# Summing a residual gate in 16 double pieces, and moving the last stages' tiles by 64 bytes

## The chip, the cores and the metric

The kernel runs on one core of one Trainium2 chip. The metric is the device time of one execution in microseconds; the smaller, the better. Engines are named as in the profile: PE (TensorE, with PEld for its weight loads), DVE (VectorE), ACT (ScalarE), POOL (GpSimd) and SP (SyncE, which issues all the DMAs of this kernel).

## What is computed

One layer of a diffusion backbone on 256 latent and 256 context tokens, 2048 channels wide, in f32:

```
sh_x, sc_x, g_x = split(silu(c) @ w_mod + b_mod, 3)        # the residual gate is g_x, 2048 numbers
hm   = rmsnorm(h) * (1 + scale) + shift                    # latents and context
u    = hm @ w_in    # r, k, v, z, decay, a | q, kv, k_rope, z | merge gates
y    = rwkv7_scan(...) over context then latents, both directions, 16 heads
o_rw = groupnorm(y) + bonus, gated by silu(z)
o_ml = attention of latents over latents + context, gated by silu(z)
m    = sigmoid(mg_r) * (o_rw @ w_br_r) + sigmoid(mg_m) * (o_ml @ w_br_m)
out  = x + g_x * (m @ w_out)
```

## The kernel before

Every big product is made of three matmuls in the float32r type, high part times high part, high times low and low times high (`mm3`, L222). Weights come in 512 KB tiles `w` of a pool with three buffers (`NW`). The generator `weights` (L211) loads one and splits it in two halves, `wh` on ACT and `wl` on DVE. A projection tile (`proj_g`, L359) takes two such loads and makes 48 matmuls of 256 columns for the latents alone, or of 512 for latents and context.

The first stage (to about 137 us) makes the modulation and the normed input `hmh`, `hml`. Then comes the recurrence: 16 halves (8 head pairs, context then latents), each with a `front` that prepares it, a `diagonal` that inverts 16x16 blocks by way of small DRAM tiles (`dl`, `ln`, `dw`, `WT`), and a `back` that carries the state. A planner (`drive`, with a modelled clock) weaves these chains with a background of projection tiles while the program is written; the framework then orders each engine's queue by its own estimate of readiness. Attention follows, then the branch stage (`chp`, 768 matmuls of 256 columns, from 1168 us) and the output stage (`ch`, `lv`, 384 of 512 columns).

The residual gate needs `silu(c) @ w_mod_g`. It is cut in 8 column blocks `b` by 4 row groups `r`. Each piece is one load of 512 KB and four matmuls that lie side by side in TensorE, into the unused half of a projection tile's `acc` bank. `gate_add` sums the pieces of a block in `gacc` on DVE; `gate_sum` (two small matmuls and an addition) makes two columns of `gT`. When all 8 blocks are there, `gd<-gT` stores `gT` transposed to DRAM (2048 runs of four bytes), from where the output stage reads it back as `gx`. The store is written behind the attention in the program; the framework puts it where it becomes ready.

In the program as built, the tiles `hmh` and `hml` begin 64 bytes past a multiple of 128 in each partition, `w`, `wh` and `wl` on a multiple of 128, and so do `ob0h` to `ob1l` (the branches' inputs), `mh` and `mlo` (the merged tile, high and low part).

Of the kernel before, what the change touches and what calls it, by code (L numbers as in the profile page):

```python
# [9 lines left out]
F32 = mybir.dt.float32  # L10
# [6 lines left out]
P = 128  # L17
D = 2048
KT = D // P
T = 256  # L20
# [32 lines left out]
NW, NSP, UN, NWM = 3, 3, 2, 11  # L53
# [74 lines left out]
def hybrid_block(  # L128
# [20 lines left out]
    nc = tc.nc  # L149
    clock = Clock()  # L150
    V, S = Elementwise(nc.vector, clock, 960, 0.066), Elementwise(nc.scalar, clock, 1200, 0.08)
    E = Tensor(nc.tensor, clock)
# [3 lines left out]
    wp = ctx.enter_context(tc.tile_pool(name="wp", bufs=2))  # L156
# [28 lines left out]
    ssil = cst.tile([P, KT, 32], F32, name="ssil")  # L185
# [17 lines left out]
    def halfs(pool, shape, name, bufs=2):  # L203
        return [pool.tile(shape, F32R, name=name + c, tag=name + c, bufs=bufs) for c in "hl"]
# [39 lines left out]
    with tc.tile_pool(name="p1", bufs=2) as p1:  # L244
# [43 lines left out]
        for k in range(KT):  # L288
# [3 lines left out]
            else:  # L292
                V.tensor_tensor(sq, xT[:, k], xT[:, k], ALU.mult)
            g = k % 4
            E.matmul(pst[32 * g:32 * g + 32], lhsT=con("ones")[:, 0:32], rhs=sq, start=k < 4, stop=k >= KT - 4,
                     tile_position=(0, 32 * g))
# [62 lines left out]
    def proj_g(tile_i, n):  # L359

        ps = pp.tile([P, 512], F32, name="acc", tag="acc", bufs=2)
        gate = None
        for q in range(2):
            if not q and n == T and gate_left:
                gate = gate_mm(ps[:, T:TT])
                yield
            for i, (wh, wl) in enumerate(weights(w_proj[tile_i, q], 1024)):
                for k in range(4):
                    cs = slice(128 * k, 128 * k + 128)
                    kk = 8 * q + 4 * i + k  # L370
                    mm3(ps[:, 0:n], wh[:, cs], wl[:, cs], hmh[:, kk, 0:n], hml[:, kk, 0:n], kk == 0, kk == KT - 1)
                    if n > T or k % 2:
                        yield
            if gsum:
                gate_sum()
        if gate:
            gate_add(ps[:, T:TT], *gate)
        return ps[:, 0:n]
# [1 line left out]
    gT = cst.tile([P, KT], F32, name="gT")  # L380


    gate_left = [(b, r) for b in range(8) for r in range(4)]
    gacc = wp.tile([P, T], F32, name="gacc", bufs=1)
    gsum = []

    def gate_mm(ps):

        b, r = gate_left.pop(0)
        wg = wp.tile([P, 4, T], F32, name="w", tag="w", bufs=NW)  # L390
        nc.sync.dma_start(wg, w_mod_g[b, r])
        for g in range(4):
            E.matmul(ps[32 * g:32 * g + 32], lhsT=ssil[:, 4 * r + g], rhs=wg[:, g], start=True, stop=True,
                     tile_position=(0, 32 * g))
        return b, r

    def gate_add(ps, b, r):
        if r:
            V.tensor_tensor(gacc, gacc, ps, ALU.add)
        else:  # L400
            V.tensor_copy(gacc, ps)
        if r == 3:
            gsum.append(b)

    def gate_sum():
# [898 lines left out]


    mg = ctx.enter_context(tc.tile_pool(name="mg", bufs=2))
    ob = [halfs(mg, [P, 8, T], f"ob{b}", 1) for b in range(2)]
    orw = mg.tile([P, 8, T], F32, name="orw", bufs=1)
    for b in range(2):
# [7 lines left out]
    while gate_left:  # L1317
        ps = pp.tile([P, 512], F32, name="acc", tag="acc", bufs=2)
        gate_add(ps[:, 0:T], *gate_mm(ps[:, 0:T]))
# [6 lines left out]
    for j in range(KT):  # L1326
        tm = []
        for b in range(2):
            th = mg.tile([P, T], F32, name=f"gth{b}")
            nc.sync.dma_start(th, thd[16 * b + j])  # L1330
            ps = pp.tile([P, 512], F32, name="chp", tag="ch", bufs=2)
# [150 lines left out]
```

## Time and profile before

| what | value |
|---|---|
| time, median of 3 runs | 1366.77 us (1360.61 to 1370.45) |
| the profiled execution's own time | 1353.92 us |
| its span, first to last instruction | 1351.9 us |
| mean granted TensorE clock | 0.997 |
| PE / PEld / DVE / ACT busy | 1312.3 / 1076.7 / 945.6 / 622.1 us |
| gate pieces | 32 loads, 32 sums on DVE |

PE busy is the union of its matmuls' spans; gaps are what is left. "idle before" and the bracket at a row's end tell how long the engine had stood before it and which instruction let it go. PEclk is the clock that was granted, 1.00 being full. In the timeline a plain f32 matmul of the program shows as two records, so four gate matmuls are `x8`.

### The profile page before, as it was taken

To read this page: it belongs to the slowest core of one execution; us is meant where nothing else is said; L and a number is where in the kernel's file an instruction comes from. 1 tells how busy PE (TensorE), PEld (TensorE's weight loads), DVE (VectorE), ACT (ScalarE), POOL (GpSimd) and SP (SyncE) were. 2 spreads that over 40 slices of the span, in tenths; PEclk is the share of its full clock that TensorE was granted. 3 is DMA by queue.
4 is the path that set the end of the run, shared out by engine and by line. 5 is a ranking of instruction groups with operands and counts; after the bars stand their busy time and mean duration, and the time that the engine had idled before them with its cause. 6 is when DMAs were issued, how large, how long until landed. Compare 5 with 4: busy or idle time off the path is not lost. (4 is left out here: it accounts for less than half of the span.)

```text
span 1351.9 us, 29680 instructions
## 1 busy us (share of the span) xinstructions
PE 1312.3 (97%) x11522; PEld 1076.7 (80%) x11522; DVE 945.6 (70%) x2675; ACT 622.1 (46%) x1370; POOL 3.3 (0%) x9
## 2 busy tenths in 40 slices
PE   5999999999999999999999998999999999999998
PEld 1767877787777877877877887876998888999887
DVE  3444988777877877787687685663488777677655
ACT  2444554444434544444435343433465565444443
POOL 0000000000000000000000000000000000000000
PEclk9999999999999999999999998999999999999999
DMA  9995564244322433433433453321743334877585
GB/s 369 417 388 199 187 175 108 69 143 131 90 77 77 122 96 94 125 91 103 125 83 103 122 138 91 103 83 56 226 149 125 101 95 139 267 227 224 197 270 174
DMA packets 127741, 208.13 MB, mean 154 GB/s; under 512 B 63600, under 2 KB 80752, under 8 KB 127088
## 3 DMA queue, kind: packets, MB, share of 16 engines
q1 hardware_dynamic: 127600, 206.23, 48.7%
q8 instruction: 91, 1.49, 0.5%
q14 instruction: 50, 0.41, 0.1%
HBM read 193.33 MB, written 12.85 MB: 153 GB/s over the span
## 5 line engine op out<-in xcount | busy, mean ns | idle before, releaser
L123 ACT CAST wh<-w 128x512 fp32r<-128x512 f32 (+2 forms) x484 | 291.4, 607 | 327.2 <-PE acc L104 143.8
L123 DVE TENSOR_TENSOR wl<-w,wh 128x512 fp32r<-128x512 f32 (+1 forms) x480 | 322.0, 676 | 168.7 <-ACT wh L123 140.8
L104 PE MATMUL acc<-hmh,wh 128*128 128x256 f32 (+1 forms) x1200 | 385.7, 322 | 0.2 <-ACT wh L123 0.2
L104 PE MATMUL acc<-hml,wh 128*128 128x256 f32 (+2 forms) x1200 | 369.4, 308 | 0.0
L104 PE MATMUL acc<-hmh,wl 128*128 128x256 f32 (+1 forms) x1184 | 364.4, 308 | 1.3 <-DVE wl L123 1.2
L104 PEld LDWEIGHTS acc<-hmh,wh 128*128 128x128 f32 x1200 | 225.8, 188 | 29.4 <-issue 9.1
L104 PEld LDWEIGHTS acc<-hmh,wl 128*128 128x128 f32 x1184 | 222.9, 188 | 15.2 <-DVE wl L123 2.3
L104 PEld LDWEIGHTS acc<-hml,wh 128*128 128x128 f32 (+1 forms) x1200 | 225.3, 188 | 11.1 <-issue 0.2
L123 ACT COPY UV<-Mn 64x128 f32<-64x128 f32 x112 | 33.1, 295 | 33.8 <-DVE Mn L123 32.5
L123 ACT COPY UV<-chp 64x128 f32<-64x128 f32 x64 | 16.5, 258 | 61.9 <-PE chp L104 61.6
L123 DVE TENSOR_TENSOR pr<-wt 64x14 f32<-64x14 f32 (+6 forms) x224 | 42.4, 189 | 2.6
L123 DVE TENSOR_TENSOR wt<-wt,pr 64x14 f32<-64x14 f32 (+6 forms) x224 | 42.2, 188 | 2.5
L123 DVE COPY xs<-chp 128x128 f32<-128x128 f32 x64 | 18.5, 288 | 35.3 <-PE chp L104 33.4
L104 PE MATMUL pm<-wm,ssil 128*32 128x256 f32 x512 | 34.9, 398 | 8.2 <-DMA wm<-in_w_mod_ss 8.1
L104 PEld LDWEIGHTS chp<-UV,AQ 128*64 128x64 f32 (+1 forms) x512 | 24.9, 135 | 19.7 <-issue 6.4
L104 PE MATMUL a<-hmh,wh 128*128 128x512 f32 x96 | 40.6, 423 | 0.0
L104 PEld LDWEIGHTS chp<-UV,BKT 128*64 128x64 f32 x448 | 24.4, 136 | 20.1 <-issue 8.8
L123 DVE SCALAR_TENSOR_TENSOR Mn<-chp,rho,Mr 128x64 f32<-128x64 f32 x96 | 23.5, 279 | 23.9 <-PE chp L104 23.7
L104 PE MATMUL wk<-QR,BK 64*128 64x128 f32 x256 | 37.2, 286 | 2.8 <-DVE QR L123 2.8
L104 PE MATMUL a<-hmh,wl 128*128 128x512 f32 x96 | 38.0, 396 | 0.0
L104 PE MATMUL a<-hml,wh 128*128 128x512 f32 x96 | 37.8, 394 | 0.0
L104 PE MATMUL chp<-UV,BKT 128*64 128x64 f32 x448 | 37.2, 238 | 0.6 <-ACT UV L123 0.4
(324 smaller groups left out, 2484.9 us busy)
## 6 DMA issues: line engine op xcount, KB each, us to landing
w<-in_w_proj SPq DMA_DIRECT2D x148, 512.0 KB, 3.7
wm<-in_w_mod_ss SPq DMA_DIRECT2D x64, 512.0 KB, 9.2
w<-in_w_mod_g SPq DMA_DIRECT2D x32, 512.0 KB, 3.7
w<-in_w_br SPq DMA_DIRECT2D x32, 512.0 KB, 4.3
w<-in_w_out SPq DMA_DIRECT2D x32, 512.0 KB, 3.9
w<-in_w_first SPq DMA_DIRECT2D x16, 384.0 KB, 7.4
xT<-in_xcT SPq DMA_DIRECT2D x4, 1024.0 KB, 12.5
thd<-th SPq DMA_DIRECT2D x32, 128.0 KB, 2.3
```

The lines of the kernel that those rows point to most:

```text
L104: return self.engine.matmul(out, lhsT=lhsT, rhs=rhs, **kw)
L123: return fn(out, *a, **kw)
```

## The change

Each gate piece now takes two loads and eight matmuls: the two groups of four add up in the accumulator, so there are 16 pieces, 16 sums on DVE, and half as many projection tiles carry one. And a tile of 16 floats per partition, `shift`, which nothing uses, is allocated ahead of `ob`, so the tiles of the branch and output stages (`ob`, `orw`, `mh`, `mlo`, `gx` and the small ones) begin 64 bytes further on, 64 past a multiple of 128. `w`, `wh` and `wl` stay.

```diff
-    gate_left = [(b, r) for b in range(8) for r in range(4)]
+    gate_left = [(b, r) for b in range(8) for r in range(2)]
...
         b, r = gate_left.pop(0)
-        wg = wp.tile([P, 4, T], F32, name="w", tag="w", bufs=NW)
-        nc.sync.dma_start(wg, w_mod_g[b, r])
-        for g in range(4):
-            E.matmul(ps[32 * g:32 * g + 32], lhsT=ssil[:, 4 * r + g], rhs=wg[:, g], start=True, stop=True,
-                     tile_position=(0, 32 * g))
+        wgs = []
+        for i in range(2):
+            wgs.append(wp.tile([P, 4, T], F32, name="w", tag="w", bufs=NW))
+            nc.sync.dma_start(wgs[i], w_mod_g[b, 2 * r + i])
+        for i in range(2):
+            for g in range(4):
+                E.matmul(ps[32 * g:32 * g + 32], lhsT=ssil[:, 4 * (2 * r + i) + g], rhs=wgs[i][:, g], start=i == 0, stop=i == 1,
+                         tile_position=(0, 32 * g))
...
-        if r == 3:
+        if r == 1:
             gsum.append(b)
...
     mg = ctx.enter_context(tc.tile_pool(name="mg", bufs=2))
+
+    mg.tile([P, 16], F32, name="shift", bufs=1)
     ob = [halfs(mg, [P, 8, T], f"ob{b}", 1) for b in range(2)]
```

The planner sees other matmuls, so the whole order of the recurrence shifts. Three places matter below. The first is SP's queue where the projections begin; `w<-in_w_mod_g` is a gate load, `w<-in_w_proj` a weight load, and the number behind a name is that of the buffer's use. Before:

```order
L391 DMA w_1478<-in_w_mod_g 128x1024
L214 DMA w_1484<-in_w_proj 128x1024
L214 DMA w_1518<-in_w_proj 128x1024
L391 DMA w_1558<-in_w_mod_g 128x1024
L214 DMA w_1564<-in_w_proj 128x1024
```

Now:

```order
L393 DMA w_1484<-in_w_mod_g 128x1024
L393 DMA w_1486<-in_w_mod_g 128x1024
L214 DMA w_1496<-in_w_proj 128x1024
L214 DMA w_1530<-in_w_proj 128x1024
L393 DMA w_1577<-in_w_mod_g 128x1024
L393 DMA w_1579<-in_w_mod_g 128x1024
```

Four loads per tile now share the three buffers, where it was three; each load takes the buffer of the third load ahead of it, so `w_1530`, a tile's second weight load, takes that of `w_1484`, its first gate load.

The second place is the store of the gate on SP. Before, it stood in the fifteenth half's part, ahead of that half's `dl` and `ln`:

```order
L978 DMA orwd_1298<-y_9684 128x256
L1323 DMA gd_14602<-gT_1289 128x16x1
L214 DMA w_10420<-in_w_proj 128x1024
L795 DMA dl_10178<-AQ_10040 16x8x16 x8
L421 DMA thd_1293<-th_10256 128x256
L214 DMA w_10570<-in_w_proj 128x1024
L798 DMA ln_10248<-dl_10178 64x256
```

Now it stands behind the eighth half's `ln` and ahead of `th<-in_wup`, the small weights of the next pair's decay and gate projections:

```order
L801 DMA ln_5699<-dl_5643 64x256
L214 DMA w_6121<-in_w_proj 128x1024
L214 DMA w_6170<-in_w_proj 128x1024
L1328 DMA gd_14587<-gT_1289 128x16x1
L214 DMA w_6234<-in_w_proj 128x1024
L636 DMA th_6018<-in_wup 128x256
L424 DMA thd_1293<-th_5920 128x256
L819 DMA dw_5785<-wt_5751 64x2x256
```

The store has moved forward by some 180 SP instructions and has other neighbours.

The third place is DVE where that load is used: `wal<-th,wah` is the low part of `th`; `W` (in the code `W2`) and `xs` belong to the `back` chain. Before, in a pair's row:

```order
L123 COPY xs<-chp 128x128
L123 TENSOR_TENSOR wt<-wt,pr 64x8x7
L123 SCALAR_TENSOR_TENSOR rs_z<-rs_y 128x8
L123 TENSOR_TENSOR wal<-th,wah 128x256
L123 TENSOR_TENSOR pr<-wt 64x7x8
L123 TENSOR_TENSOR rs_z<-rs_z,nrm 128x8
```

Now, for the load behind the store:

```order
L123 SCALAR_TENSOR_TENSOR rs_z<-rs_y 128x8
L123 TENSOR_TENSOR wal<-th,wah 128x256
L123 TENSOR_TENSOR wt<-wt,pr 64x3x12
L123 TENSOR_TENSOR W_5850<-WT_1302,lv 128x512
L123 TENSOR_TENSOR pr<-wt 64x2x13
L123 TENSOR_TENSOR rs_z<-rs_z,nrm 128x8
L123 COPY xs<-chp 128x128
```

`W` and `xs`, which the `back` chain's next matmuls need, have come to stand behind `wal`.

## The prediction

> **What bounds the kernel.** I read the page first: its span, the busy times and the chain that ended last.
>
> ```profile
> span 1351.9 us, 29680 instructions
> PE 1312.3 (97%) x11522; PEld 1076.7 (80%) x11522; DVE 945.6 (70%) x2675; ACT 622.1 (46%) x1370; POOL 3.3 (0%) x9
> PE 34%; DMA 3%; DVE 3%; ACT 1%; issue 1%; DVEq 0%; ACTq 0%; SPq 0%
> ```
>
> TensorE is occupied for 97% of the span and leads the chain (which can't be followed past the branch stage's dense part, so its shares do not add up to 100%). So only three things can move the time: TensorE's own work, its 1351.9 - 1312.3 = 39.6 us of gaps, and its clock. Next I read the stretches that the change touches.
>
> ```profile
> core 0: us, PE busy (x) PEld busy (x) DVE busy (x) ACT busy (x) POOL busy (x), PEclk, DMA share, GB/s
> 137.00:200.00 63.00, 59.98 (x506) 52.45 (x502) 55.42 (x151) 30.63 (x62) 1.44 (x4) 1.00 0.59 186
> 200.00:440.00 240.00, 237.43 (x2336) 184.77 (x2337) 183.65 (x578) 104.59 (x253) 0.00 (x0) 1.00 0.36 101
> 800.00:850.00 50.00, 43.30 (x455) 38.34 (x453) 34.85 (x101) 21.38 (x51) 0.00 (x0) 0.93 0.41 111
> ```
>
> From 137 to 440 us, where the gate's loads will now be crowded, TensorE idles for 3.0 and 2.6 us. The largest hole is at 800 to 850: 6.7 us idle, and the only stretch here whose clock falls below 1.00. The SP queue's rows in order of time show who made it.
>
> ```profile
> 808.27 0.92 SPq L1323 DMA_DIRECT2D gd<-gT  x1
> 810.61 0.34 SPq L214 DMA_DIRECT2D w<-in_w_proj  x1
> 811.21 12.31 SPq L795 DMA_DIRECT2D dl<-AQ  x8
> ...
> 825.40 0.46 SPq L798 DMA_DIRECT2D ln<-dl  x1
> ```
> ```profile
> gd<-gT SPq DMA_DIRECT2D x1, 8.0 KB, 13.0
> ```
> ```profile
> 829.36 0.67 DVE L123 COPY wt<-ln 32x256 f32<-32x256 f32 x2 [3.61 <-DMA ln<-dl]
> ...
> 831.86 0.69 DVE L123 TENSOR_TENSOR Z<-lv,cc 128x512 f32<-128x512 f32 x1
> ...
> 832.60 1.65 PE L104 MATMUL lv<-WT,Z 64*64 64x64 f32 x26 [5.85 <-DVE Z L123]
> ```
>
> The gate's transposed store, only 8 KB, takes 13.0 us to land, and the eight `dl` stores behind it take 12.31 us to issue. `ln` comes late, VectorE stands in `wt<-ln` and cannot reach `Z`, and TensorE waits 5.85 us. It then runs slow:
>
> ```profile
> 835.27 0.56 PE L104 MATMUL acc<-hmh,wh 128*128 128x256 f32 x1
> ...
> 836.48 0.41 PE L104 MATMUL acc<-hmh,wl 128*128 128x256 f32 x1
> ```
>
> Five spacings in 1.21 us are 0.24 us each, about twice the pace of other stretches. Of the clock, 0.07 x 50 = 3.5 us is lost; about 1 us of that falls into the wait itself, so the loss is 2.5 us and the hole costs 8.3 us in all.
>
> **Term 1, half as many gate sums.** A gate's four matmuls cost TensorE their own time and two changes of stream.
>
> ```profile
> 159.34 0.28 PE L104 MATMUL acc<-hmh,wl 128*128 128x256 f32 x1
> 159.54 0.64 PE L104 MATMUL acc<-w,ssil 128*32 128x256 f32 x8
> 160.11 0.39 PE L104 MATMUL acc<-hmh,wh 128*128 128x256 f32 x1
> ```
> ```profile
> 61.25 1.93 PE L104 MATMUL pm<-wm,ssil 128*32 128x256 f32 x32
> ```
>
> From the projection matmul ahead of the gate to the one behind it pass 0.77 us, against 0.113 without a gate: 0.66 us for one set. Four sets in a row (the `pm` row: same shapes) take 1.93 us against 0.64 for one, so each added set costs 0.43. Joining two saves 0.66 - 0.43 = 0.23 us, and sixteen joins save **3.6 us**. Bounds: nothing, if the second load is not there in time (term 4), and 5.3 us (16 x 0.33) if the exit shrinks too.
>
> On VectorE sixteen additions go.
>
> ```profile
> L123 DVE TENSOR_TENSOR gacc<-gacc,acc x24: 406/421/422, 151.9 to 788.2; 128x256 f32<-128x256 f32 x24
> ACT th L123 <- DVE gacc L123: 15.1, 13, 2.2
> ```
>
> That is 16 x 0.42 = 6.7 us and about half of ScalarE's 15.1 us of waiting. Both engines have slack beside TensorE, so I count nothing; if TensorE weren't the cover, at most 6.7 us would come back.
>
> **Term 2, the store `gd` moves.** The sums are now complete near the eighth half of the recurrence, not the fourteenth. The store leaves the place above, which frees 8.3 us, and lands two rows ahead of the load `th<-in_wup`. What waits there is seen one pair later in the trace of before:
>
> ```profile
> 583.75 0.43 SPq L633 DMA_DIRECT2D th<-in_wup  x1
> 587.40 0.40 ACT L123 CAST wah<-th 128x256 fp32r<-128x256 f32 x1 [1.79 <-DMA th<-in_wup]
> 589.56 0.41 DVE L123 TENSOR_TENSOR wal<-th,wah 128x256 fp32r<-128x256 f32 x1
> ```
>
> ScalarE already waits for this load, which takes 3.6 us; VectorE needs it 5.8 us after its issue. Behind the store it lands like the `w` of 810.61, 12.6 us after issue, some 9 us late. After 2.2 us of slack VectorE stands 7 us at `wal`, with `W2` and `xs` behind it in the order, for which TensorE waits; TensorE has about 1.5 us queued ahead. So 5.5 us idle and again 2.3 us of clock: 7.8 us. Net **-0.5 us**. Bounds: -8.3, if the order of before and after leaves enough work ahead, and +4, if VectorE's backlog counts too. I take the middle, since the nearest row, the hole of before, has the same make. SP itself stands at the store until the last `gT` is written, and behind it also wait the spill `thd` and the store `dw`; I count nothing for `dw`, because the inversion that feeds it is held at `wal` as well.
>
> **Term 3, the 64 bytes.** Two rows of one unbroken stream in the timeline, with the number of matmuls between them, give the pace of a matmul; the rows with x768 and x96 are the chain's.
>
> ```profile
> 975.83 0.28 PE L104 MATMUL acc<-hml,wh 128*128 128x256 f32 x1
> ...
> 979.00 0.28 PE L104 MATMUL acc<-hmh,wl 128*128 128x256 f32 x1
> ```
> ```profile
> 799.06 0.28 PE L104 MATMUL acc<-hmh,wh 128*128 128x256 f32 x1
> ...
> 802.94 0.28 PE L104 MATMUL acc<-hmh,wh 128*128 128x256 f32 x1
> ```
> ```profile
> 1168.21 92.15 PE chp L104 x768
> ...
> 1282.24 21.76 PE lv L104 x96
> ```
> ```profile
> 600.53 0.39 PE L104 MATMUL acc<-hmh,wh 128*128 128x512 f32 x1
> ...
> 607.53 0.39 PE L104 MATMUL acc<-hmh,wh 128*128 128x512 f32 x1
> ```
>
> With moving tiles at 64 past a multiple of 128 (`hmh`, `hml`) and weights on a multiple, 256 columns take 3.17 / 28 = 0.113 us in most streams and 3.88 / 33 = 0.118 in some. In the branch stage both lie on a multiple, and the pace is 92.15 / 768 = 0.120. With 512 columns it is the reverse: 7.00 / 30 = 0.233 in the first relation, 21.76 / 96 = 0.227 in the output stage, where both lie on a multiple. The change gives both stages the first relation. The branch stage then gains 768 x 0.0067 = **5.1 us** (1.8 at the pace 0.118), the output stage pays 384 x 0.0066 = **2.5 us** (nothing, if only the moving tile counts, since there it is the stationary one that shifts). Nothing covers either: TensorE has no gaps there.
>
> [...]
>
> **Term 4, three buffers for four loads.** Before, the one gate tile's buffer is free a whole tile ahead. Now the tile's second weight load takes the buffer of its own gate load, so it is issued only when that gate has run.
>
> ```profile
> w<-in_w_mod_g SPq DMA_DIRECT2D x32, 512.0 KB, 3.7
> ```
> ```profile
> L123 ACT CAST wh<-w 128x512 fp32r<-128x512 f32 (+2 forms) x484 | 291.4, 607 | 327.2 <-PE acc L104 143.8
> L123 DVE TENSOR_TENSOR wl<-w,wh 128x512 fp32r<-128x512 f32 (+1 forms) x480 | 322.0, 676 | 168.7 <-ACT wh L123 140.8
> ```
> ```profile
> 136.65 0.64 PE L104 MATMUL acc<-w,ssil 128*32 128x256 f32 x8
> ...
> 190.15 0.64 PE L104 MATMUL acc<-w,ssil 128*32 128x256 f32 x8 [0.23 <-ACT th L123]
> ```
>
> Gate 0.7, landing 3.7, issue 0.3, the two halves of a split 0.6 + 0.7: ready 6.0 us after the tile's start. A tile takes (190.15 - 136.65) / 6 = 8.9 us here, of which 48 x 0.113 = 5.4 are its own matmuls, 0.7 its gate and 2.8 other work. TensorE wants the second load after 1.1 + 2.7 + 1.4 = 5.2 us: 0.8 us short. Queued behind it on SP stand the next gate's loads and the next first load, which is ready some 1 us late too; the two overlap in part. Seven tiles at about 1 us, less the 3.0 us of gaps that fall together with it, cost **4 us**. Bounds 0 and 12. After 200 us a tile has about as much other work as its own, so the remaining nine are covered; without that cover each costs 1 to 2.6 us.
>
> **Sum.** -3.6 - 0.5 - 5.1 + 2.5 + 4 = -2.7 us: the profiled execution would go from 1353.92 to 1351.2. The median shown, 1366.77, lies 0.95% above that execution; I take the same difference off it: **1364 us**.
>
> **Rivals.**
> - The store's new place is covered: work queued on TensorE hides the late load, and VectorE's stand costs nothing there. For it: the rest of the recurrence loses only 1 us in 100. Against: ScalarE already waits for this load. Term 2 becomes -8.3: 1356 us.
> - The shift does nothing (the pace follows from how a stream is entered, as the 0.113 and 0.118 of equal tiles hint). [...] Terms 1, 2 and 4 remain: 1366.6 us.
> - On the other side: the loads starve all sixteen double tiles. If other work between gate and second load stays under 1.4 us, each tile pays 1.0 us for its second load and 1.6 us for the next first one: 16 x 2.6 = 42 us in place of 4, and the time is 1402 us. For it: three buffers, four loads a tile. Against: DMA is busy to 0.36 only, and chains fill half of TensorE after 200 us.
>
> **Chances.** Forecast 0.56, covered store 0.18, idle shift 0.15, starved tiles 0.09, none of these 0.02. The range, with the ends of terms 2 to 4 and half a per cent for the runs, is 1350 to 1380. A measurement of this kernel tells about 1% from no change: below 1353 lie a quarter of the covered store and a fifth of the forecast's spread, 0.17; above 1380 the starved tiles and a few slow ends, 0.12; between, 0.71.
>
> **What would show it.** Gate rows `acc<-w,ssil x16` of about 1.05 us (term 1). `gd<-gT` near the middle of the span, `wah` and `wal` late by 7 us behind it, one halved clock there and none near 830 (term 2). `chp` of x768 in 87 us and the four output blocks at 22.4 us each (term 3). More PE idle between 137 and 200, released by `wh` or `wl` (term 4). I'm wrong if a new long wait stands elsewhere in the reshuffled order, or if the branch stage keeps its 92 us.

## The result, and the profile after

| what | before | after |
|---|---|---|
| median of 20 runs each | 1358.78 us (1353.45 to 1370.45) | 1367.59 us (1362.45 to 1378.30) |
| ratio to before, 95% interval | | 1.0056 [1.0031, 1.0080] |
| profiled execution, its span | 1353.92, 1351.9 us | 1367.96, 1365.8 us |
| mean granted clock in that execution | 0.997 | 0.984 |

By the ratio, the change makes the kernel 0.56% slower, about 7.6 us; the two medians lie 8.8 us apart. The forecast was 2.7 us less. The median lies inside the range that was given, but the sign is wrong. The first lines of the page after:

```profile
span 1365.8 us, 29667 instructions
...
PE 1316.4 (96%) x11522; PEld 1083.3 (79%) x11522; DVE 942.8 (69%) x2659; ACT 620.2 (45%) x1370; POOL 3.3 (0%) x9
```

Of the 13.9 us between the two spans 9.8 are gaps of TensorE (49.4 us against 39.6) and 4.1 are longer busy time, though there is less to do. The table of stretches says where; its columns are as in the prediction. First three stretches of before, then the kernel after:

```profile
200.00:240.00 40.00, 39.95 (x419) 31.42 (x420) 32.42 (x98) 17.80 (x41) 0.00 (x0) 1.00 0.39 105
...
440.00:600.00 160.00, 159.19 (x1655) 127.14 (x1652) 122.81 (x410) 72.00 (x174) 0.00 (x0) 1.00 0.37 107
...
960.00:1020.00 60.00, 59.51 (x446) 55.41 (x447) 43.56 (x125) 34.61 (x70) 0.00 (x0) 1.00 0.59 182
```
```profile
137.00:200.00 63.00, 56.28 (x443) 47.91 (x442) 50.65 (x134) 28.17 (x58) 3.09 (x5) 0.92 0.55 181
200.00:240.00 40.00, 37.26 (x355) 30.43 (x354) 25.49 (x88) 13.69 (x30) 0.00 (x0) 0.91 0.48 141
...
440.00:600.00 160.00, 154.58 (x1631) 125.70 (x1631) 117.57 (x361) 71.58 (x173) 0.00 (x0) 0.99 0.39 104
...
800.00:850.00 50.00, 48.28 (x459) 42.66 (x459) 38.94 (x127) 25.98 (x62) 0.00 (x0) 1.00 0.48 140
...
960.00:1020.00 60.00, 57.34 (x417) 54.82 (x416) 37.38 (x103) 30.83 (x62) 0.00 (x0) 0.91 0.61 184
```

From 137 to 240 us TensorE now idles 6.7 + 2.7 us; before it was 3.0 and 0.05. The clock, 1.00 in both stretches before, is 0.92 and 0.91. The hole at 800 to 850 is gone (1.7 us idle in place of 6.7), and one has come between 440 and 600 (5.4 us in place of 0.8). A last one, at 974, has half clock behind it. In all, the clock stood at one half for 30.7 us between 137 us and the output stage's end, before for 6.8. Three places in the timeline, the first at the second tile that carries a joined piece:

```profile
140.13 0.33 SPq L214 DMA_DIRECT2D w<-in_w_proj  x1
140.57 0.85 SPq L393 DMA_DIRECT2D w<-in_w_mod_g  x2
145.67 3.24 SPq L214 DMA_DIRECT2D w<-in_w_proj  x2
```
```profile
144.35 1.30 DVE L123 TENSOR_TENSOR wl<-w,wh 128x512 fp32r<-128x512 f32 x2 [0.59 <-ACT wh L123]
...
150.44 1.14 ACT L123 CAST wh<-w 128x512 fp32r<-128x512 f32 x2 [1.51 <-DMA w<-in_w_proj]
```
```profile
147.88 1.07 PE L104 MATMUL acc<-w,ssil 128*32 128x256 f32 x16
151.10 0.39 PE L104 MATMUL acc<-hmh,wh 128*128 128x256 f32 x1 [2.15 <-ACT wh L123]
```

The gate's two loads hold two of the three buffers. So the tile's first weight load goes out only at 145.67, when `wl` of the tile before is done (144.35 + 1.30) and the third comes free. It lands just ahead of `wh` at 150.44; TensorE runs the 16 gate records, then stands for 2.15 us. That is the shortage of buffers that term 4 spoke of, but on the tile's first load, for which it had counted some 1 us. Not every early gap is of this kind:

```profile
218.77 0.41 PE L108 MATMUL wk<-cc,rnb 128*128 128x128 f32 x2 [1.95 <-DVE rnb L123]
```

Of the 9.5 us idle from 137 to 240 us, the waits over 0.4 us for `wh` and `wl` make 4.8; this one and another behind it, for VectorE's `W`, make 2.7, and no load ends either. The second place is the store:

```profile
498.27 0.38 SPq L1328 DMA_DIRECT2D gd<-gT  x1
499.65 1.25 SPq L214 DMA_DIRECT2D w<-in_w_proj  x1
500.94 0.43 SPq L636 DMA_DIRECT2D th<-in_wup  x1
```
```profile
508.75 0.67 PE L104 MATMUL chp<-UV,AQ 64*64 64x64 f32 x4 [1.93 <-issue]
...
513.00 0.40 ACT L123 CAST wah<-th 128x256 fp32r<-128x256 f32 x1 [6.48 <-DMA th<-in_wup]
513.44 0.42 DVE L123 TENSOR_TENSOR wal<-th,wah 128x256 fp32r<-128x256 f32 x1 [6.50 <-ACT wah L123]
...
514.99 0.45 PE L104 MATMUL chp<-xs,W 64*64 64x64 f32 x8 [1.80 <-DVE xs L123]
```

The load `th<-in_wup` lands 12.1 us after its issue, ScalarE stands 6.48 us, VectorE 6.50 us at `wal`, and `xs` is late for TensorE: the prediction's chain, link by link. The third place had not been foreseen:

```profile
974.92 0.68 DVE L123 TENSOR_TENSOR krw<-krw 64x512 f32<-64x512 f32 x1 [4.18 <-DMA krw<-krd]
975.53 0.67 DVE L123 TENSOR_TENSOR wl<-w,wh 128x512 fp32r<-128x512 f32 x1
976.25 0.38 PE L104 MATMUL acc<-hmh,wl 128*128 128x256 f32 x1 [2.48 <-DVE wl L123]
```

A small load of the attention's keys is late, VectorE stands at it with a `wl` behind it. With joined pieces and no 64 bytes the same gap was 0.90 us in one profiled execution and 2.04 in another (the two kernels `pair_only` and `pair_cheap` below), so its size changes between executions. Last, the chain:

```profile
1181.25 90.46 PE chp L104 x768
...
1294.18 22.40 PE lv L104 x96
```

The branch stage takes 1.7 us less than before (92.15), the output blocks 0.64 us more each (21.76).

### The profile page after: what moved, and what is told of

It reads as the page before. It is cut to its first block, busy times and chain, and to the rows that moved or that the text cites. A ratio compares the mean times of both kernels' runs of the same rounds, so it can differ in the third digit from the quotient of the medians.

```text
span 1365.8 us, 29667 instructions
## 1 busy us (share of the span) xinstructions
PE 1316.4 (96%) x11522; PEld 1083.3 (79%) x11522; DVE 942.8 (69%) x2659; ACT 620.2 (45%) x1370; POOL 3.3 (0%) x9
## 5 line engine op out<-in xcount | busy, mean ns | idle before, releaser
L104 PE MATMUL acc<-hmh,wh 128*128 128x256 f32 (+1 forms) x1200 | 390.1, 325 | 3.9 <-ACT wh L123 3.9
L104 PE MATMUL acc<-hmh,wl 128*128 128x256 f32 (+1 forms) x1184 | 369.6, 312 | 5.7 <-DVE wl L123 5.7
L104 PEld LDWEIGHTS acc<-hmh,wh 128*128 128x128 f32 x1200 | 230.4, 192 | 27.0 <-ACT wh L123 4.8
L104 PEld LDWEIGHTS acc<-hmh,wl 128*128 128x128 f32 x1184 | 227.4, 192 | 20.2 <-DVE wl L123 7.5
L104 PEld LDWEIGHTS acc<-hml,wh 128*128 128x128 f32 (+1 forms) x1200 | 229.7, 191 | 10.0 <-issue 0.2
L104 PE MATMUL chp<-UV,AQ 128*64 128x64 f32 (+1 forms) x512 | 36.9, 236 | 2.8 <-issue 2.2
L123 DVE TENSOR_TENSOR AQ<-wk,cc 128x256 f32<-128x256 f32 (+1 forms) x48 | 24.5, 511 | 16.9 <-PE wk L104 16.1
```

The lines of the kernel that those rows point to most:

```text
L104: return self.engine.matmul(out, lhsT=lhsT, rhs=rhs, **kw)
L123: return fn(out, *a, **kw)
```

## The experiments

All ratios are to the kernel before on the same chip. "Idle" is that of TensorE from 137 to 240 us, "half clock" the time at a granted clock of 0.5 from 137 us to the end of the output stage, both of the profiled execution; "clock" is the median of the granted clock over the runs. The kernel before had 0.991 to 0.992 in the same batches.

| kernel | ratio, 95% interval | idle, us | half clock, us | clock |
|---|---|---|---|---|
| before | 1 | 3.1 | 6.8 | 0.992 |
| the change | 1.0056 [1.0031, 1.0080] | 9.5 | 30.7 | 0.986 |
| `shift_only` | 0.9997 [0.9970, 1.0023] | 3.0 | 6.8 | 0.992 |
| `pair_only` | 1.0056 [1.0031, 1.0082] | 11.0 | 20.5 | 0.984 |
| `pair_oneload` | 1.0030 [1.0003, 1.0057] | 2.8 | 30.7 | 0.984 |
| `before_cheap` | 0.9949 [0.9926, 0.9971] | 3.0 | 23.9 | 0.994 |
| `pair_cheap` | 0.9990 [0.9969, 1.0010] | 10.9 | 17.1 | 0.989 |
| `pair_late_cheap` | 1.0033 [1.0015, 1.0052] | 5.3 | 23.9 | 0.987 |
| `before_skip1` | 1.0031 [1.0011, 1.0052] | 9.5 | 23.9 | 0.988 |
| `pair_oneload_cheap` | 0.9970 [0.9949, 0.9992] | 2.8 | 17.1 | 0.987 |
| `pair_alt_cheap` | 0.9941 [0.9912, 0.9969] | 4.0 | 0.0 | 0.991 |
| `best_a` | 0.9967 [0.9941, 0.9993] | 4.6 | 0.0 | 0.991 |
| `best_b` | 0.9922 [0.9892, 0.9952] | 4.0 | 3.4 | 0.994 |

### The two halves of the change

`shift_only` is the kernel before with one line more, `pair_only` the changed kernel without it:

```diff
+    mg.tile([P, 16], F32, name="shift", bufs=1)
     ob = [halfs(mg, [P, 8, T], f"ob{b}", 1) for b in range(2)]
```

> The kernel before with the 64 bytes alone; the order of the work is the same. Theory 1 (the change's loss is new gaps of TensorE and the halved clock behind them, all from the reordered recurrence): the branch stage's 768 matmuls take 87 to 90.5 us in place of 92.15, the four output blocks 22.4 in place of 21.8 each, together 0 to -3 us and +2.5, so the time stays within 2 us of the kernel before; PE idle before the branch stage is unchanged. Rival 2 (the shift itself is what costs): +6 to +9 us, as the whole change. Rival 3 (the shift does nothing): branch stage 92.1, output blocks 21.8.

> The whole change without the 64 bytes: joined gate pieces alone. Theory 1 (gaps and halved clock): 6 to 9 us slower than before, with the gaps at 149, 182, 217, 507, 513 and 974 us as in the changed kernel and windows of half clock behind them; branch stage back at 92 us, output blocks at 21.8. Rival 2 (the shift costs): no slower than before.

The chain of `shift_only`:

```profile
1171.44 90.45 PE chp L104 x768
...
1284.37 22.40 PE lv L104 x96
```

And of `pair_only`:

```profile
1177.56 92.14 PE chp L104 x768
...
1291.59 21.76 PE lv L104 x96
```

The 64 bytes do what they did in the whole change, -1.7 and +2.5 us, and the time does not tell it from nothing. VectorE's instructions come in the same order as before in `shift_only`, and as in the changed kernel in `pair_only`. The loss is that of the joined pieces alone.

### The store, at its old and at its new place

`before_cheap` and `pair_cheap` replace the store in the kernel before and in `pair_only`:

```diff
-    nc.sync.dma_start(gd.rearrange("c p -> p c"), gT)
+    pt = pp.tile([P, 512], F32, name="acc", tag="acc", bufs=2)
+    E.transpose(pt[0:KT, 0:P], gT, con("ident"))
+    gr = mg.tile([KT, P], F32, name="gr", bufs=1)
+    S.copy(gr, pt[0:KT, 0:P])
+    nc.sync.dma_start(gd, gr)
```

> The kernel before, with the gate transposed on TensorE first and stored in 16 runs of 512 bytes, late, in place of 2048 runs of four bytes at 808 us. Theory 1: the gap of 5.85 us at 827 and the half clock behind it go, the rest of the order stays; 6 to 8.5 us faster than before. Rival 5 (the store only takes the blame, the eight dl stores take 12 us there anyway): dl takes 12 us again and the gap stays; 0 to 1 us.

> Joined pieces without the 64 bytes, and the gate transposed on TensorE and stored late in 16 runs of 512 bytes, so nothing is stored at 498 us. If the store's new place has its price (term 2 of the prediction): the waits of TensorE at 507 to 517 us (4.5 us together) and the half clock behind them go, 4 to 7 us under the joined kernel, a ratio to before of about 1.001. If it was covered there, or if every order of the recurrence loses the same: still 1.0056.

The stretch that held the hole, in `before_cheap`:

```profile
800.00:850.00 50.00, 49.21 (x517) 44.12 (x515) 42.04 (x124) 27.29 (x64) 0.00 (x0) 1.00 0.44 128
```

0.8 us idle in place of 6.7, and the eight `dl` stores issue in 3.64 us in place of 12.31:

```profile
822.67 3.64 SPq L795 DMA_DIRECT2D dl<-AQ  x8
```

VectorE's order is that of before, and the kernel is 0.51% or 6.9 us faster: the store did make the hole. At the new place it goes from 1.0056 to 0.9990, 0.66% or 9.0 us (by the two intervals some 4 to 13). The cheap store also stands elsewhere, at 1174 and 1173 us, behind the recurrence; what 16 runs would cost at the old places is not shown. In `pair_cheap` the stretch from 440 to 600 us is whole:

```profile
440.00:600.00 160.00, 159.25 (x1715) 130.63 (x1715) 122.50 (x380) 74.71 (x181) 0.00 (x0) 1.00 0.36 107
```

The move of the store was thus about even within these intervals, as forecast; and joining without the slow store still loses 0.4% against `before_cheap`.

### The loads, and the order

In `pair_oneload`, made from `pair_only`, the second four matmuls read the first load; `pair_oneload_cheap` is the same with the cheap store; `pair_late_cheap` lets the pieces begin at the ninth tile; `pair_alt_cheap` puts them on every second tile.

```diff
-            wgs.append(wp.tile([P, 4, T], F32, name="w", tag="w", bufs=NW))
-            nc.sync.dma_start(wgs[i], w_mod_g[b, 2 * r + i])
+            wgs.append(wgs[0] if i else wp.tile([P, 4, T], F32, name="w", tag="w", bufs=NW))
+            if not i:
+                nc.sync.dma_start(wgs[0], w_mod_g[b, 2 * r])
...
             if not q and n == T and gate_left:
+                gate_turn[0] += 1
+            if not q and n == T and gate_left and gate_turn[0] > 8:       # pair_late_cheap
+            if not q and n == T and gate_left and gate_turn[0] % 2:       # pair_alt_cheap
```

> Joined pieces as in the kernel above, but the second set of four matmuls reads the first load again: half of the gate's weights are never loaded, so the gate that comes out is another one. A tile then has three loads for three buffers, as before. Theory 1a (the crowded loads make the early gaps): PE idle from 137 to 240 us falls from about 9 to about 3 us, no wait for wh or wl over 1 us there, the windows of half clock there go, and the time is 10 to 14 us under the joined kernel. Rival 4 (any new order of the recurrence costs some us, whatever the loads): idle and half-clock windows of the same size remain at some place, and the time is within 4 us of the joined kernel.

> Joined pieces, cheap late store, and the second set of four matmuls reads the first load again (half of the gate's weights are never loaded, the gate is another one). Against the joined kernel with the cheap store, whose ratio to before was 0.999, only the sixteen extra loads are gone. If they make the early gaps (term 4): PE idle from 100 to 250 us 3 us in place of 10.9, the clock loss smaller too, ratio 0.990 to 0.995. If the order of the recurrence makes them: the ratio stays between 0.997 and 1.001.

> The kernel above, with the joined pieces beginning at the ninth tile that could carry one, once the chains take half of TensorE. If four loads on three buffers in the first tiles make the early gaps (term 4): PE idle from 137 to 240 us about 3 us in place of 10, 4 to 10 us under the kernel above, a ratio to before of 0.994 to 0.998. If the order of the recurrence, whatever the loads, sets gaps and clock: the mean granted clock stays at 0.984 and the time within 3 us of the kernel above.

> Joined pieces on every second tile that could carry one, cheap late store: as many gate loads per us as before. If four loads on three buffers cost only where they follow tile by tile: idle from 100 to 250 us under 6 us and a ratio of 0.993 to 0.997. If each joined tile pays at its place whatever the spacing, or the new order pays elsewhere: 0.999 to 1.004.

Two stretches each, first `pair_cheap`, then `pair_oneload_cheap`:

```profile
137.00:200.00 63.00, 54.83 (x448) 45.98 (x447) 51.07 (x138) 29.54 (x60) 3.10 (x5) 0.96 0.59 190
200.00:240.00 40.00, 37.25 (x344) 30.90 (x343) 23.55 (x76) 12.29 (x27) 0.00 (x0) 0.85 0.44 135
```
```profile
137.00:200.00 63.00, 60.43 (x515) 51.93 (x513) 55.08 (x142) 31.53 (x63) 3.09 (x5) 1.00 0.55 171
200.00:240.00 40.00, 39.77 (x358) 30.01 (x357) 30.66 (x102) 18.02 (x41) 0.00 (x0) 1.00 0.39 109
```

Without the sixteen extra loads the early idle falls from 10.9 to 2.8 us and the clock there is whole; with the plain store it falls from 11.0 to 2.8 us, but 10.2 us of half clock stay, from 196 us on. Twice the early gaps went with the loads. That the loads alone make them is not shown: without them VectorE's instructions come in another order from 138 us on, so loads and order changed together, and `before_skip1` below has 9.5 us of early idle with single pieces. The loads' part is what the rows at 145.67 to 151.10 show. The time gains less than both expectations, 3.5 us where 10 to 14 stood with the plain store and 2.7 where 5 to 12 stood with the cheap one, by intervals that reach zero. The median clock did not come back with the loads gone (0.984 with them and without them with the plain store, 0.989 and 0.987 with the cheap one): it fell elsewhere, in `pair_oneload_cheap` between 240 and 440 us, where it is 0.96 with 2.9 us idle.

The late start missed its expectation. It has half the early idle, but new gaps later:

```profile
552.64 0.39 PE L104 MATMUL acc<-hmh,wh 128*128 128x256 f32 x1 [0.99 <-ACT wh L123]
...
557.65 0.38 PE L104 MATMUL acc<-hmh,wh 128*128 128x256 f32 x1 [1.50 <-ACT wh L123]
...
612.92 1.19 PE L104 MATMUL wk<-Qbd,BK 128*128 128x128 f32 x4 [2.94 <-DVE BK L123]
```

Only the first is for a load: ScalarE stood 2.66 us at `wh` for it. The other two come from VectorE's `BK`, at 557 by way of ScalarE, where `wh` stands behind an instruction that waits 3.25 us for `BK`. So the chains of the middle do not quite cover four loads on three buffers either, and the new order costs more there. Every second tile does, as expected: 4.0 us idle, no half clock from 137 us to the output stage's end in that execution, 0.9941. Beside `before_cheap`, which keeps the single pieces (0.9949), that is no gain that the intervals tell from nothing: what joining saves on TensorE does not show in the time.

The control `before_skip1` has all 32 single pieces, from one tile later on:

```diff
             if not q and n == T and gate_left:
+                gate_turn[0] += 1
+            if not q and n == T and gate_left and gate_turn[0] > 1:
```

> The kernel before, with the 32 single pieces beginning one tile later and nothing else: no work is added or taken away, but the planner's order changes. If any new order costs some us in gaps and clock: 4 to 9 us slower than before. If the loss of the change is that of its loads and its store: within 3 us of before.

```profile
174.91 3.63 PE L104 MATMUL wk<-Qbd,BK 128*128 128x128 f32 x16 [4.25 <-DVE BK L123]
...
198.65 0.93 PE L104 MATMUL wk<-cc,gacc 128*128 128x2 f32 x4 [4.04 <-DVE gacc L123]
```

This change of order costs 0.31%, 4.2 us (by the interval 1.5 to 7.1, so the second expectation, under 3, is not excluded). VectorE has three `wl` ahead of the last `BK` and three ahead of `gacc`. It is one order among many; a rewrite that changes the planner's order is to be read against this size.

### What a gap costs

`holes` is `before_cheap` with five waits in the dense branch stage: the first matmul of blocks 2, 5, 8, 11 and 14 waits for a chain of 3, 6, 9, 13 and 20 copies on VectorE (`n` and two more).

```diff
+    HOLES = {2: 1, 5: 4, 8: 7, 11: 11, 14: 18}
...
+            n = HOLES.get(j, 0)
+            if n and not b:
+                hd = mg.tile([P, 64], F32, name="hd")
+                V.tensor_copy(hd, prev[:, 0:64])
+                for _ in range(n):
+                    V.tensor_copy(hd, hd)
+                V.tensor_copy(ps[:, 0:64], hd)
```

> The kernel before with the cheap late store, and five waits put into the dense branch stage: the first matmul of blocks 2, 5, 8, 11 and 14 waits for a chain of 3, 6, 9, 13 and 20 small VectorE copies, some 0.5, 1, 1.6, 2.4 and 3.6 us. If a gap of TensorE is what brings the half clock: no window of half clock behind the shortest, one of 3.4 us or more within 4 us behind the longest two, and the limit lies between 1 and 2 us; each such gap costs its length and 1.7 us or more. If the half clock has nothing to do with gaps: the windows fall elsewhere, and each gap costs its length alone.

One row for each gap, in order:

```profile
1166.00:1187.00 21.00, 19.35 (x159) 18.98 (x159) 14.96 (x33) 9.08 (x16) 0.00 (x0) 1.00 0.70 230
1187.00:1208.00 21.00, 18.46 (x140) 18.08 (x139) 13.53 (x33) 8.15 (x15) 0.00 (x0) 0.92 0.58 184
1208.00:1229.00 21.00, 17.77 (x134) 17.39 (x134) 13.54 (x34) 7.54 (x14) 0.00 (x0) 0.92 0.56 167
1229.00:1252.00 23.00, 18.73 (x136) 18.36 (x135) 14.23 (x38) 7.97 (x15) 0.00 (x0) 0.85 0.52 165
1252.00:1282.00 30.00, 24.13 (x187) 23.76 (x187) 20.64 (x56) 10.80 (x20) 0.00 (x0) 0.89 0.52 161
```

In the first row, with 1.65 us idle (0.74 + 0.91, a few matmuls between), the clock stayed at 1.00. With 2.5 and 3.2 us idle it was 0.92 over 21 us, 3.4 us of half clock each; with 4.3 and 5.9 it was 0.85 over 23 us and 0.89 over 30, some 6.8 us each. The stage grew from 92.1 to 118.7 us: 17.6 us of gaps and 9.0 us of clock.

The traces of before and of the change, from 137 us to the output stage's end, show the same. Five waits of TensorE that began at full clock took 1.93 us or more: 5.85 us (ahead of 832.60) in before; 2.15 (151.10), 1.95 (218.77), 1.93 (508.75) and 2.48 (976.25) in the change. Inside the first, and 0.9 to 1.8 us behind the end of the others, at 831.14, 151.97, 220.24, 510.37 and 978.00, the clock went to one half, for 6.8, 3.4, 6.8, 3.4 and 3.4 us. In the change it also did so for 3.4 us at 169.04, behind waits of 0.83 and 0.87 us, and at 189.52, with 1.09 us idle in the 3.4 us ahead. The longest waits at full clock that no half clock followed within 3.5 us are 1.32 us (183.18) and 1.19 (310.85) in the change, 1.05 (187.96) in before.

Two stretches of half clock in the change, 3.4 us each at 984.82 and 995.06, follow no idle time: TensorE was busy for all of the 3.4 us ahead of each. Matmuls of two columns stand there, ahead of the second these:

```profile
991.83 1.05 PE L104 MATMUL wk<-cc,sq 128*128 128x2 f32 x8
...
993.66 1.05 PE L104 MATMUL wk<-cc,sq 128*128 128x2 f32 x8
```

They count as busy, at 0.13 us for each of the eight records. That the clock takes them for idle time is my guess and not shown: no run varied them, and in before the same matmuls stand at 979.73 and 981.56 us in a stretch (960 to 1000) whose clock is 1.00.

### The address

Tiles that nothing uses move the branches' and the merged tiles, in `before_cheap` or, for `best_b`, in `pair_alt_cheap`. The edit of `offsets`; the others differ in the numbers of floats:

```diff
-    ob = [halfs(mg, [P, 8, T], f"ob{b}", 1) for b in range(2)]
+    mg.tile([P, 8], F32, name="shift", bufs=1)
+    ob = [halfs(mg, [P, 8, T], "ob0", 1)]
+    mg.tile([P, 16], F32, name="shift2", bufs=1)
+    ob.append(halfs(mg, [P, 8, T], "ob1", 1))
...
+    mg.tile([P, 8], F32, name="shift3", bufs=1)
     mh = mg.tile([P, KT, T], F32R, name="mh", bufs=1)
```

> The kernel before with the cheap late store, and the 64 bytes for the branches' tiles alone: the merged tiles mh and mlo are put back on a multiple of 128. If the pace follows the address of the moving and the stationary tile: branch stage 90.5 us or less, output blocks 21.8, and 7 to 9 us faster than before (ratio 0.993 to 0.995). If the output stage's slower pace came from something else that the change moved: output blocks 22.4.

> The kernel before with the cheap late store; the tiles of branch 0 begin 32 bytes past a multiple of 128, those of branch 1 96 bytes past it, mh and mlo on a multiple. The 384 matmuls of each branch are read apart. If only the halves of 128 bytes count: 0.120 us for branch 0 and 0.113 to 0.118 for branch 1. If any offset between moving tile and weights does: both 0.113 to 0.118. If the address does not set the pace: both 0.120.

> The kernel before with the cheap late store; the tiles of branch 0 begin 128 bytes past a multiple of 256, those of branch 1, mh and mlo 192 bytes past one. So far the branch stage took 0.1200 us a matmul at 0 (mod 256), 0.1178 at 64, 0.1183 at 32 and 0.1197 at 96; the output stage 0.2267 at 0, 0.2333 at 64, 0.2323 at 128. If the pattern has a period of 256 bytes or more: branch 1 at 0.113 to 0.114, as the projections, whose hmh and hml lie at 192. If its period is 128: branch 0 at 0.120 and branch 1 at 0.1178, and the output stage at 0.2333. If the pace hangs on how a stream is entered and not on the address: 0.120 and 0.2267.

> Joined pieces on every second tile, the cheap late store, the branches' tiles at 192 bytes past a multiple of 256, and mh and mlo on a multiple of 256. If address and spacing both do as the runs so far say: the branch stage at 87 us (0.1133 a matmul) or 90.5 (0.1178), the output blocks at 21.8, and 3 to 5 or 1.7 us under the kernel with joined pieces on every second tile (ratio 0.9941): 0.990 to 0.993. If the pace hangs on how a stream is entered: 92.15 us and 0.994.

`best_a` is `before_cheap` with `ob` alone shifted and `mh` and `mlo` on a multiple of 128. Its ratio, 0.9967, missed what was expected, and its output stage stayed slow:

```profile
1164.44 90.45 PE chp L104 x768
...
1277.30 22.31 PE lv L104 x96
```

So the pattern of the prediction, 64 against 0 modulo 128, does not hold: `mh` lay on a multiple of 128 and the block took 22.31 us, not 21.76. In the program as built it had come to lie at 128 modulo 256, in before at 0. By the tiles' places modulo 256 the chains give, for the branches' 256 columns, 0.1200 us at 0 (before) and 0.1178 at 64 (the change, `shift_only`, `best_a`); for the output stage 0.2267 at 0 (before), 0.2333 at 64 (the change, `shift_only`), 0.2323 at 128 (`best_a`, `offsets`) and 0.2289 at 192 (`offsets2`). The projections' `hmh`, with the fastest pace (0.113 in most streams of before), lies at 192. In the two kernels whose branches lay apart (one execution each) no expectation was met to the digit: the chain's 768 matmuls took 91.28 us in `offsets` (32 and 96), 0.1189 each, and 90.19 us in `offsets2` (128 and 192), 0.1174 each, and there the rows of the branch at 192 stand 0.117 us apart from 1199.80 to 1201.09. `best_b` is `pair_alt_cheap` with both branches' tiles at 192 and `mh`, `mlo` at 0:

```profile
1163.48 87.06 PE chp L104 x768
...
1272.45 21.76 PE lv L104 x96
```

0.1134 us a matmul and a stage 5.1 us shorter than before, with the output stage's blocks at 21.76 us as in before, and VectorE's order that of `pair_alt_cheap`. That is what was expected. Why the place should matter no run shows. By the ratios it is 2.6 us under `pair_alt_cheap`, within the intervals. It is the fastest of all: 0.9922, about 10.6 us under the kernel before. Against the changed kernel, through the ratios, it is 1.3% faster.

## Why the prediction was wrong

- **The baseline.** The profiled execution of before, with a clock of 0.997 and no half clock at 30 us (the change's has 10.2 us of it there, as most later executions have), was faster than all but one of the twenty runs, and the three runs shown had a median 8 us above that of the twenty. So 1364 us came near the measured 1367.6 by luck, counted down from a median that was too high.
- **Term 1** (3.6 us) held in size per join. The 16 gate records take 1.07 us, forecast 1.05. From the projection matmul ahead to the one behind pass 1.207 us, less 0.113 that is 1.09 for a joined set against 2 x 0.66: 0.23 us a join. In four of the sixteen pieces (at 281, 392, 444 and 470 us) other work stands between the gate's matmuls, so the term is nearer 12 x 0.23 = 2.8 us. What VectorE saves did not show, as expected.
- **Term 2** (-0.5 us) held in its mechanism, both ways: the old place cost 6.9 us (8.3 forecast), the new one 9.0 (7.8). The net is +2, inside its bounds, and by the intervals not told from the forecast.
- **Term 3** (-2.6 us) failed by its value for the branch stage: I took the pace 0.113, it was 0.1178, the bound, so -1.7 and not -5.1; the output stage's +2.5 was exact. With it the term is +0.8. The step behind it, that the place modulo 128 decides, did not hold (`best_a`, output blocks at 22.31 us); with both branches' tiles at 192 modulo 256 the 5.1 us are there (`best_b`, 87.06 us). What sets the pace is not shown, nor why some projection streams with the same tiles took 0.118.
- **Term 4** (+4 us, bounds 0 and 12) was right about the buffers, but it priced an idle us as a us. Idle from 137 to 240 us rose by 6.4 us (3.1 to 9.5). In the hole at 827 I had counted the clock; here I left it out, and from 151.97 to 227.06 us four stretches of half clock came, 17.1 us together, each with 1.1 to 2.4 us idle in the 3.4 us ahead. By my estimate, half of their length less the 0.8 us idle in them, that is up to 8 us more, double the term. That the loads bring this clock loss is not shown: without them the time falls by 3.5 and 2.7 us, near the 4 forecast, and the clock stays as low. The cover claimed after 200 us was not whole either (`pair_late_cheap`).
- **Not in the sum at all:** that a new order of the recurrence costs something by itself, in gaps and in the clock behind them. One tile's delay cost 4.2 us. The 974 gap belongs here.

With terms 2 and 3 as measured and the rest as forecast, the sum is -3.6 + 2 + 0.8 + 4 = +3.2 us in place of -2.7: the pace that I took for the branch stage is enough to lose the sign. The other 4.4 of the 7.6 us lie in what the sum left out, the clock behind the new gaps and the cost of a new order. How they share it stays open.

Of the rivals, the covered store did not come about; the idle shift was nearer in size (+0.8 in place of 0) than the forecast; the starved tiles were right in their mechanism, a fifth of their 42 us in idle time (8 us, if all of it is the loads') and under a tenth in time. An estimate of the clock's share takes from each run's time half of its half clock, the part of the span that the granted clock fell short of 1. The medians are then 1346.2 us for the kernel before (35 runs beside `shift_only`; the clocks of the twenty are not on record), 1348.1 for the changed one and 1345.2 for `pair_only` in the batch of those 35. By that nearly all of the loss would be the clock. But in the two traces 34 us more of half clock (10 of it near 30 us) went with only 4.1 us more busy time, 6.8 once the gate's 3.5 and the address's 0.8 are taken out, and 9.8 us more of gaps. Why 6.8 is less than half of 34 I did not settle; idle time under the half clock explains little of it (1.4 of the 30.7 us). So both shares are there, and their sizes are open.

## What to carry to other kernels

Price a gap of a bound TensorE with the clock behind it: in `holes`, gaps of 2.5 us and more cost their length and some 1.5 us for each 3.4 us of half clock (9.0 us for 20.4), while 1.65 us in two gaps left the clock at 1.00. Joining transfers into fewer, larger pieces saves instructions and crowds the buffers: spread the pieces so that loads per buffer turnover stay as they were (every second tile gained 0.5% over every tile, and nothing measurable over not joining). Have a control for the order, where a planner sets it. And the store of 2048 four-byte runs was paid by the transfers queued behind it, at both places where it stood (the eight `dl` stores issued in 12.31 us, 3.64 without it; `th<-in_wup` landed 12.1 us after its issue, 3.6 one pair later in before); transposing it first, which also took it behind the recurrence, gained 6.9 and 9.0 us.

## What the runs showed of the hardware that I had not expected

- Half clock came behind short gaps: 3.4 us of it behind 2.5 and 3.2 us idle, 6.8 behind 4.3 and 5.9, none behind 1.65 (`holes`); in the change 3.4 or 6.8 us behind single waits of 1.93 to 2.48 us, and 3.4 us behind 0.83 + 0.87. At 984.82 and 995.06 it came with no idle time in the 3.4 us ahead, where two-column matmuls stood.
- Equal matmul streams had other paces in kernels whose tiles begin at other places modulo 256 bytes: for 256 columns 0.1200 us at 0 (before), 0.1178 at 64 (the change) and 0.1134 at 192 (`best_b`), for 512 columns 0.2267 at 0 (before) and 0.2333 at 64 (the change). In `offsets2` rows of a branch at 192 stand 0.117 apart, where `best_b` has 0.113, so something else counts too.
- The same kernel's time varies by 1.3% from run to run (1353.45 to 1370.45), and over the changed kernel's twenty runs it follows the granted clock: 1362.5 us at 0.987 to 0.990, 1378.3 at 0.979.
